# The value projections of mLSTM heads 0 and 1 joined into 512-column matmuls and moved behind the second FoX head pair's q and k

## The chip, the cores and the metric

The kernel runs on one core of one Trainium2 chip. The metric is the device time of the program in microseconds (us), the median of three runs. A profiled execution, taken separately, gives the trace that is read below. Engines are named as in the profile: PE is TensorE's matmul, PEld its weight load, DVE is VectorE, ACT is ScalarE, POOL is GpSimd, SP issues most DMAs.

## What is computed

One residual block on 512 tokens of width 1024. Cut to what matters here:

```python
proj = einsum('bsd,de->bse', h, w_in) + b_in        # h = LN(x) scaled and shifted
fq, fk, fv, ff, mu, mv, mi, mf, mo, ga, gb = split(proj)
att = forgetting_attention(fq, fk, fv, ff)          # FoX: 8 heads x 64, causal softmax
u  = silu(causal_conv(mu))
mq, mk = per head: u_head @ w_mq, u_head @ w_mk     # 4 heads, 256 -> 128
hm = mlstm_chunkwise(mq, mk, mv, mi, mf)            # 4 heads, v width 256
y  = (sigmoid(ga) * (att @ w_pa) + sigmoid(gb) * (head_norm(hm) * sigmoid(mo)) @ w_pb) @ w_out
```

followed by a layer norm and a SwiGLU of inner width 2816. `mv` is the value projection of the mLSTM branch: 512 x 1024 (tokens by d_model) times 1024 x 256 for each of four heads.

## The kernel before

Every float32 product is made of three matmuls on values split into a high and a low part: `mm3` issues hi x hi (L186), hi x lo (L189) and lo x hi (L190) into one PSUM bank. Weights come in chunks of 128 x 1024 (512 KB): `emit_chunk` issues the load on SP (L152, tile `raw`, three buffers), ACT casts the high part (L157, `whi`, four buffers), DVE subtracts it to make the low part (L161, `wlo`, four buffers). Chunks are taken in the order of the list `PLAN`, three ahead of their use, so a chunk's number (`whi17`, `raw17`) is its place in that list.

The stretch that the change touches is the FoX phase (about 77 to 222 us). For each FoX head `fox_scores` makes four score tiles `fs{h}_{qb}` of 128, 256, 384 and 512 keys (L641 to L643, computed at least 256 wide) in the two PSUM banks named `s`. DVE reads each into SBUF with the forget bias and the row minimum (L646, tile `L{h}_{qb}`), which frees the bank, ACT takes the exponential (L648), DVE the reciprocal of the sum (L649), ACT scales (L650). `fox_out` transposes the tiles on PE (L663), ACT copies them (L665, `pT`) and PE multiplies with `v` (L671, `fo`).

Projections fill PE between these steps. They are generators in the list `queue`: `prep_u(h)` (mu and the convolution), `prep(h)` (the values of an mLSTM head, then its `mqk`), `fm_unit` (a block of fq, fk, mo). `fill(n)` runs the next n pieces of the first ones. All projections, and `mqk`, write to the two PSUM banks named `acc`, so a unit waits until DVE or ACT has read the unit before the last out of its bank. For fq that is two ACT copies (L301) and two DVE subtractions (L302, tiles `ql`), one for each head of the pair; for fk the same (L310, L311). The tiles of q and k of a head have two buffers, so the pair 2 overwrites the pair 0.

`prep(0)` makes, for each of four token blocks, 8 x 3 matmuls with 256 moving columns (the head's value width), adds the bias on DVE (L614, `vt`) and splits the sum into `vxh` and `vx`. After the FoX phase `ml_scores` loads a row of `rowd` broadcast over partitions (tile `nb`, issued by ACT, L704) and the mLSTM phase follows.

The code's order is not the order on the engines: the framework's scheduler places every instruction, from the dependences and its own idea of time. The rows of both programs are therefore shown with the change.

Of the kernel before, what the change touches and what calls it, by code (L numbers as in the profile page):

```python
# [8 lines left out]
F32 = mybir.dt.float32  # L9
# [3 lines left out]
ALU = mybir.AluOpType  # L13
# [3 lines left out]
P = 128  # L17
D = 1024
S = 512
KT = 8  # L20
# [22 lines left out]
def plan():  # L43
    out = [("start", k) for k in range(KT)]
    out += [("gv", j) for j in range(4)]

    def mu(h):
        return [("mu", 2 * h), ("mu", 2 * h + 1)]

    def mvqk(h):  # L50
        return [("mv", 2 * h), ("mv", 2 * h + 1), ("mqk", h)]

    out += mvqk(0)
    out += [("fq", 2), ("fk", 2)]
    out += mu(1) + mvqk(1)
    out += [("fq", 3), ("fk", 3)]
    out += mu(2)
    out += [("mo", 0), ("mo", 1)]
    out += mu(3)
    out += [("mo", 2), ("mo", 3)]  # L60
    out += mvqk(2)
    out += [("mo", 4), ("mo", 5)]
    out += mvqk(3)
    out += [("mo", 6), ("mo", 7)]
    for f in range(8):
        out += [("ga", f), ("gb", f), ("pa", f)]
        if f > 0:
            out += [("pb", f - 1)]
    out += [("pb", 7)]
    out += [("wo", k) for k in range(KT)]  # L70
    for f in range(FT):
        out += [("fg", f), ("fu", f)]
    for q in range(4):
        out += [("dn", q * 6 + j) for j in range(6)]
    return out
# [25 lines left out]
def block_kernel(ctx, tc, x, c, wada, wpk, cols, gvb, mvb, lnp, out):  # L101
    nc = tc.nc
    V, A, G, T = nc.vector, nc.scalar, nc.gpsimd, nc.tensor
# [27 lines left out]
    offs = {}  # L131
# [4 lines left out]
    st = {"n": 0, "tiles": {}, "resident": {}}  # L136
    AHEAD = 3

    def w_off(key):

        if key[0] in ("gv", "mv") or key in (("fg", 0), ("fu", 0), ("fg", 1), ("fu", 1)):
            return 0
        return 16

    def emit_chunk(i):
        key = PLAN[i]
        w = chunk_width(key)
        if key in (("wo", 6), ("wo", 7), ("fu", 1), ("fg", 2)):
            raw = adap.tile([P, VW], F32, tag="adaw", name=f"raw{i}", bufs=2)
        else:  # L150
            raw = stp.tile([P, CW], F32, tag="raw", name=f"raw{i}", bufs=3)
        st["dma"] = nc.sync.dma_start(raw[:, :w], wpk[offs[key]:offs[key] + P * w].rearrange("(p w) -> p w", p=P))  # L152
        if key in st["resident"]:
            hi, lo = st["resident"][key]
        else:
            hi, lo = (stp.tile([P, CS], F32R, tag=t_, name=f"{t_}{i}")[:, w_off(key):w_off(key) + w] for t_ in ("whi", "wlo"))
        st["hi"] = A.copy(hi[:, :w], raw[:, :w])  # L157
        if key in LATE_LO:
            late.append((lo[:, :w], raw[:, :w], hi[:, :w]))
        else:  # L160
            (G if key in POOL_LO else V).tensor_tensor(lo[:, :w], raw[:, :w], hi[:, :w].bitcast(F32), ALU.subtract)  # L161
        st["tiles"][key] = (hi, lo)
# [16 lines left out]
    def get(key, ahead=AHEAD):  # L179
        prefetch(key, ahead)  # L180
        return st["tiles"].pop(key)

    def mm3(ps, lhs, rhs, first, last, pin=False):
        lh, ll = lhs
        rh, rl = rhs
        m = T.matmul(ps, lh, rh, start=first, stop=False)  # L186
        if pin:
            tc.keep_in_program_order(m)
        T.matmul(ps, lh, rl, start=False, stop=False)  # L189
        T.matmul(ps, ll, rh, start=False, stop=last)  # L190

    def split(hi, lo, src):
        A.copy(hi, src)  # L193
        V.tensor_tensor(lo, src, hi.bitcast(F32), ALU.subtract)
# [41 lines left out]
    def acc_tile(name):  # L236
        return ps.tile([P, S], F32, tag="acc", name=name)
# [119 lines left out]
    for hf in range(2):  # L357
        s_ = slice(hf * S, hf * S + S)
# [25 lines left out]
    for tb in range(TB):  # L384
        xt = xts[tb]
        mv = small.tile([P, 2], F32, tag="lnmv", name=f"xmv{tb}")
# [14 lines left out]
        for h in range(2 if tb == TB - 1 else 1):  # L401
            s_ = slice(h * S, h * S + S) if tb == TB - 1 else slice(0, D)
# [10 lines left out]
    for k in range(KT):  # L413
        pt = pts[k]
        sc, sh = mods[:, 2 * k:2 * k + 1], mods[:, 2 * k + 1:2 * k + 2]
        if k == 0:
            w = start_conv(0)
# [8 lines left out]
        hi, lo = w  # L426
        if k + 1 < KT:
            w = start_conv(k + 1)
# [11 lines left out]
    mla_s, mla = scope(name="mla", bufs=2)  # L440
# [12 lines left out]
    def hk(k, sl=slice(0, S)):  # L453
        return hhi[:, k, sl], hlo[:, k, sl]
# [15 lines left out]
    queue = []  # L470
# [16 lines left out]
    mvt = {0: fox.tile([P, S], F32, tag="mvt", name="mvt0", bufs=1)}  # L487
# [68 lines left out]
    mq, mk, vx = {}, {}, {}  # L556
# [31 lines left out]
    def fm_unit(name, b):  # L588
        yield from gemm_fm(name, b)
        r = evac_fm(name, b, gemm_done.pop((name, b)))  # L590
        if name == "mo":
            mot[b] = r

    def prep_u(h):
        for i in range(2):
            b = 2 * h + i
            if b not in mup:
                yield from fm_unit("mu", b)
            conv(b)

    def prep(h):
        vl = mla.tile([P, TB, 258], F32R, tag="vx", name=f"vx{h}")
        vh = adap.tile([P, TB, 258], F32R, tag="adaw", name=f"vxh{h}", bufs=2)
        G.tensor_copy(vh[:, :, 256:258], ones[:, 0:2 * TB].rearrange("p (t o) -> p t o", o=2))
        G.tensor_copy(vl[:, :, 256:258], lfc[:, 0, 0:2 * TB].rearrange("p (t o) -> p t o", o=2))
        w0, w1 = get(("mv", 2 * h)), get(("mv", 2 * h + 1))
        for tb in range(TB):
            ps = acc_tile(f"mv{h}_{tb}")
            for k in range(KT):
                hi, lo = (w0, w1)[k // 4]  # L610
                s_ = slice((k % 4) * 256, (k % 4) * 256 + 256)
                mm3(ps[:, :256], hk(k, slice(tb * P, (tb + 1) * P)), (hi[:, s_], lo[:, s_]), k == 0, k == KT - 1)
            vt = mla.tile([P, 256], F32, tag="th", name=f"vt{h}_{tb}", bufs=1)
            V.tensor_tensor(vt, ps[:, :256], mvt[h // 2][:, (h % 2) * 256:(h % 2) * 256 + 256], ALU.add)  # L614
            split(vh[:, tb, 0:256], vl[:, tb, 0:256], vt)
            yield
        vx[h] = (vh, vl)
        hi, lo = get(("mqk", h))
        for i, dst in ((0, mq), (1, mk)):
            ps = acc_tile(f"mqk{h}_{i}")  # L620
            for k in range(2):
                s_ = slice((i * 2 + k) * P, (i * 2 + k + 1) * P)
                uh, ul = us[2 * h + k]
                mm3(ps, (hi[:, s_], lo[:, s_]), (uh, ul), k == 0, k == 1)
            t = mla.tile([P, S], F32, tag=f"qk{i}", name=f"qk{i}_{h}")
            A.copy(t, ps)
            dst[h] = t
        yield
# [44 lines left out]
                    tc.keep_in_program_order(m)  # L673

    mot = {}
    queue += [prep_u(0), prep(0), fm_unit("fq", 2), fm_unit("fk", 2), prep_u(1), prep(1)]
    queue += [fm_unit("fq", 3), fm_unit("fk", 3), prep_u(2), fm_unit("mo", 0), fm_unit("mo", 1), fm_unit("mu", 6), fm_unit("mu", 7)]
    fill(2)
    for p in range(NH // 2):
# [105 lines left out]
    for f in range(KT):  # L785
# [4 lines left out]
        hi, lo = get(("pa", f))  # L790
        for k in range(4):
            s_ = slice(k * P, (k + 1) * P)
# [302 lines left out]
    for f in range(NF0, FT):  # L1095
        b1, b26, b57, b34 = s_tile(f"p1_{f}"), acc_tile(f"p26_{f}"), o_tile(f"p57_{f}"), tr_tile(f"p34_{f}")
        h1, h2 = slice(0, HB), slice(HB, S)
        r = ftp.tile([P, 7, HB], F32, tag="r", name=f"r{f}", bufs=1)
# [171 lines left out]
```

## Time and profile before

| what | value |
|---|---|
| runs, us | 851.03, 851.63 (median), 855.49 |
| profiled execution, us | 852.84 |
| its span, us | 851.1 |
| mean granted clock of TensorE | 0.996 |
| PE busy | 828.2 us (97%) |
| PEld busy | 742.1 us (87%) |
| DVE busy | 597.9 us (70%) |
| ACT busy | 381.7 us (45%) |

Busy time is the time with an instruction in the engine. Matmuls are pipelined, so neighbouring ones overlap: a single matmul's busy time is longer than the distance between two starts. PE idles 22.9 us of the span.

### The profile page before, as it was taken

Reading aid. Unit: us, or ns where it says so; the run is one execution under the profiler, and the core shown is the slowest. Engines: PE = TensorE matmul, PEld = TensorE weight load, DVE = VectorE, ACT = ScalarE, POOL = GpSimd, SP = SyncE. Lnnn points to the kernel's source line nnn. Section 1 sums busy time; section 2 is a strip of 40 time slices with the busy share of each in tenths; the row PEclk is TensorE's granted clock in tenths of the full one; section 3 lists DMA queues with packets and bytes.
Section 4 is the critical chain, followed back from the end, with each engine's and each line's share of the span. In section 5 each row is a group of like instructions: output and inputs, shape, how many; then the busy total and the mean of one; then the engine's idle time right before and its main releaser. Section 6 shows DMA issues by size and latency. Waiting matters only on the chain.

```text
span 851.1 us, 14125 instructions
## 1 busy us (share of the span) xinstructions
PE 828.2 (97%) x5518; PEld 742.1 (87%) x5518; DVE 597.9 (70%) x1113; ACT 381.7 (45%) x606; POOL 80.6 (9%) x140
## 2 busy tenths in 40 slices
PE   6999999999889999999999999999999999999996
PEld 4889878777778888888888889999999999999996
DVE  7977546464387667776765898888888888744247
ACT  6555867674454333322243265644444444611110
POOL 2030000000021110000000221021111110000001
PEclk9999999999999999999999999999999999999999
DMA  9953331522212224876667216577877774522202
GB/s 351 371 163 99 125 100 66 145 75 62 94 57 75 75 75 155 282 258 239 242 234 256 114 50 174 141 193 189 196 176 174 195 191 131 179 88 99 95 30 100
DMA packets 46477, 130.08 MB, mean 153 GB/s; under 512 B 5293, under 2 KB 5693, under 8 KB 46410
## 3 DMA queue, kind: packets, MB, share of 16 engines
q1 hardware_dynamic: 37930, 113.97, 39.6%
q0 software_dynamic: 6752, 12.06, 8.4%
q10 hardware_dynamic: 1728, 3.15, 1.2%
q8 instruction: 43, 0.70, 0.3%
q14 instruction: 24, 0.20, 0.1%
HBM read 124.93 MB, written 2.13 MB: 149 GB/s over the span
## 4 chain that ended last, share of the span: by engine, by line
PE 91%; DVE 3%; DMA 1%; ACT 1%; issue 1%; POOL 0%; SPq 0%; DVEq 0%; ACTq 0%; POOLq 0%
PE p L189 7%; PE p L186 7%; PE p L190 7%; PE dn L186 5%; PE dn L189 5%; PE dn L190 5%; PE mo L186 2%; PE mo L189 2%; PE ga L190 2%; PE gb L186 2%; PE gb L190 2%; PE pb L190 2%; PE ga L186 2%; PE pb L186 2%; PE ga L189 2%; PE gb L189 2%
## 5 line engine op out<-in xcount | busy, mean ns | idle before, releaser
L161 DVE TENSOR_TENSOR wlo<-raw,whi 128x1024 fp32r<-128x1024 f32 (+2 forms) x94 | 106.3, 1136 | 109.0 <-ACT whi L157 101.8
L157 ACT CAST whi<-raw 128x1024 fp32r<-128x1024 f32 (+2 forms) x98 | 95.4, 980 | 179.7 <-PE dn L190 70.8
L189 PE MATMUL dn<-wlo,ah 128*128 128x256 f32 x352 | 97.3, 278 | 0.0
L186 PE MATMUL dn<-whi,ah 128*128 128x256 f32 x352 | 97.2, 278 | 0.1
L190 PE MATMUL dn<-whi,al 128*128 128x256 f32 x352 | 96.0, 278 | 0.0
L189 PE MATMUL p<-tlo,whiu 128*128 128x256 f32 x304 | 84.2, 277 | 0.0
L190 PE MATMUL p<-thi,wlou 128*128 128x256 f32 x304 | 84.2, 277 | 0.0
L186 PE MATMUL p<-thi,whiu 128*128 128x256 f32 x304 | 84.2, 277 | 0.0
L186 PEld LDWEIGHTS dn<-whi,ah 128*128 128x128 f32 x352 | 66.2, 188 | 0.3 <-ACT ah L193 0.3
L189 PEld LDWEIGHTS dn<-wlo,ah 128*128 128x128 f32 x352 | 66.2, 188 | 0.0
L190 PEld LDWEIGHTS dn<-whi,al 128*128 128x128 f32 x352 | 65.5, 188 | 0.0
L190 PE MATMUL p<-hhi,wlou 128*128 128x256 f32 x228 | 62.9, 276 | 0.0
L186 PE MATMUL p<-hhi,whiu 128*128 128x256 f32 x228 | 62.9, 276 | 0.0
L189 PE MATMUL p<-hlo,whiu 128*128 128x256 f32 x228 | 62.9, 276 | 0.0
L271 DVE CUSTOM_DVE_ANT_0 adaw<-adaw,cb 128x1024 f32<-128x1024 f32 x32 | 39.1, 1223 | 26.8 <-DMA adaw<-in_wada_dram 26.8
L190 PEld LDWEIGHTS p<-thi,wlou 128*128 128x128 f32 x304 | 57.2, 188 | 0.0
L189 PEld LDWEIGHTS p<-tlo,whiu 128*128 128x128 f32 x304 | 57.2, 188 | 0.0
L186 PEld LDWEIGHTS p<-thi,whiu 128*128 128x128 f32 x304 | 57.2, 188 | 0.0
L210 POOL TENSOR_TENSOR lnrs<-lnrs,mhalf 128x1 f32<-128x1 f32 x12 | 13.1, 1094 | 322.3 <-DVE lnrs L209 322.3
L193 ACT CAST whiu<-raws 128x1024 fp32r<-128x1024 f32 (+1 forms) x38 | 30.8, 832 | 28.6 <-DMA raws<-in_wpk_dram 14.9
L186 PEld LDWEIGHTS p<-hhi,whiu 128*128 128x128 f32 x228 | 42.8, 188 | 0.0
L190 PEld LDWEIGHTS p<-hhi,wlou 128*128 128x128 f32 x228 | 42.8, 188 | 0.0
(370 smaller groups left out, 2342.8 us busy)
## 6 DMA issues: line engine op xcount, KB each, us to landing
raw<-in_wpk_dram SPq DMA_DIRECT2D x84, 512.0 KB, 3.6
adaw<-in_wada_dram SPq DMA_DIRECT2D x48, 512.0 KB, 5.1
raws<-in_wpk_dram SPq DMA_DIRECT2D x57, 256.0 KB, 3.8
rawg<-in_wpk_dram SPq DMA_DIRECT2D x19, 512.0 KB, 3.9
raws<-in_wpk_dram POOLq DMA_DIRECT2D x38, 256.0 KB, 6.1
raw<-in_wpk_dram SPq DMA_DIRECT2D x16, 256.0 KB, 2.7
raw<-in_wpk_dram SPq DMA_DIRECT2D x8, 384.0 KB, 9.3
raw<-in_wpk_dram SPq DMA_DIRECT2D x4, 528.0 KB, 8.1
```

The costliest lines, as they stand in the source:

```text
L157: st["hi"] = A.copy(hi[:, :w], raw[:, :w])
L161: (G if key in POOL_LO else V).tensor_tensor(lo[:, :w], raw[:, :w], hi[:, :w].bitcast(F32), ALU.subtract)
L186: m = T.matmul(ps, lh, rh, start=first, stop=False)
L189: T.matmul(ps, lh, rl, start=False, stop=False)
L190: T.matmul(ps, ll, rh, start=False, stop=last)
L193: A.copy(hi, src)
L210: G.tensor_tensor(rs, rs, mhalf, ALU.pow)
L271: V.tensor_tensor_reduce(wt, wt, cb, 1.0, 0.0, ALU.mult, ALU.add, t)
```

## The change

The values of heads 0 and 1 are made together: `prep_v01` loads four weight chunks, each holding two of the eight k tiles for both heads side by side (two half-chunk DMAs of 256 KB each, 512 columns per k tile), and makes 8 x 3 matmuls with 512 moving columns for each token block, two token blocks at a time in both `acc` banks. That is 96 matmuls of 512 columns in place of 192 of 256. The bias add covers both heads at once (4 of 512 columns in place of 8 of 256); the splits stay 8 on ACT and 8 on DVE of 256 columns. `prep(0)` and `prep(1)` lose their value part and keep `mqk` as `prep_qk`. The queue and `PLAN` are put in another order: fq and fk of pair 2 come first, then `mqk` of head 0, mu of head 1, the joined values and `mqk` of head 1. Heads 2 and 3 keep their code.

```diff
--- before.py
+++ after.py
@@ -50,9 +50,8 @@
     def mvqk(h):
         return [("mv", 2 * h), ("mv", 2 * h + 1), ("mqk", h)]
 
-    out += mvqk(0)
-    out += [("fq", 2), ("fk", 2)]
-    out += mu(1) + mvqk(1)
+    out += [("fq", 2), ("fk", 2), ("mqk", 0)]
+    out += mu(1) + [("mv", j) for j in range(4)] + [("mqk", 1)]
     out += [("fq", 3), ("fk", 3)]
     out += mu(2)
     out += [("mo", 0), ("mo", 1)]
@@ -138,7 +137,7 @@
 
     def w_off(key):
 
-        if key[0] in ("gv", "mv") or key in (("fg", 0), ("fu", 0), ("fg", 1), ("fu", 1)):
+        if key[0] == "gv" or key[0] == "mv" and key[1] > 3 or key in (("fg", 0), ("fu", 0), ("fg", 1), ("fu", 1)):
             return 0
         return 16
 
@@ -149,7 +148,16 @@
             raw = adap.tile([P, VW], F32, tag="adaw", name=f"raw{i}", bufs=2)
         else:
             raw = stp.tile([P, CW], F32, tag="raw", name=f"raw{i}", bufs=3)
-        st["dma"] = nc.sync.dma_start(raw[:, :w], wpk[offs[key]:offs[key] + P * w].rearrange("(p w) -> p w", p=P))
+        if key[0] == "mv" and key[1] < 4:
+
+            j, c0 = divmod(key[1], 2)
+            r = raw[:, :w].rearrange("p (k h d) -> p k h d", k=2, h=2)
+            for h in range(2):
+                o_ = offs[("mv", 2 * h + j)]
+                src = wpk[o_:o_ + P * w].rearrange("(p k d) -> p k d", p=P, k=4)
+                st["dma"] = nc.sync.dma_start(r[:, :, h, :], src[:, 2 * c0:2 * c0 + 2, :])
+        else:
+            st["dma"] = nc.sync.dma_start(raw[:, :w], wpk[offs[key]:offs[key] + P * w].rearrange("(p w) -> p w", p=P))
         if key in st["resident"]:
             hi, lo = st["resident"][key]
         else:
@@ -598,11 +606,38 @@
                 yield from fm_unit("mu", b)
             conv(b)
 
-    def prep(h):
+    def v_tiles(h):
         vl = mla.tile([P, TB, 258], F32R, tag="vx", name=f"vx{h}")
         vh = adap.tile([P, TB, 258], F32R, tag="adaw", name=f"vxh{h}", bufs=2)
         G.tensor_copy(vh[:, :, 256:258], ones[:, 0:2 * TB].rearrange("p (t o) -> p t o", o=2))
         G.tensor_copy(vl[:, :, 256:258], lfc[:, 0, 0:2 * TB].rearrange("p (t o) -> p t o", o=2))
+        vx[h] = (vh, vl)
+        return vh, vl
+
+    def prep_v01():
+
+        ts = [v_tiles(h) for h in range(2)]
+        w = [get(("mv", j)) for j in range(4)]
+        for t2 in range(2):
+            pss = [acc_tile(f"mv01_{t2 * 2 + i}") for i in range(2)]
+            for j in range(4):
+                hi, lo = w[j]
+                for i in range(2):
+                    tb = 2 * t2 + i
+                    for k in (2 * j, 2 * j + 1):
+                        s_ = slice((k % 2) * S, (k % 2) * S + S)
+                        mm3(pss[i], hk(k, slice(tb * P, (tb + 1) * P)), (hi[:, s_], lo[:, s_]), k == 0, k == KT - 1)
+                if j % 2:
+                    yield
+            for i in range(2):
+                tb = 2 * t2 + i
+                vt = mla.tile([P, S], F32, tag="th", name=f"vt01_{tb}", bufs=1)
+                V.tensor_tensor(vt, pss[i], mvt[0], ALU.add)
+                for h in range(2):
+                    split(ts[h][0][:, tb, 0:256], ts[h][1][:, tb, 0:256], vt[:, h * 256:h * 256 + 256])
+
+    def prep(h):
+        vh, vl = v_tiles(h)
         w0, w1 = get(("mv", 2 * h)), get(("mv", 2 * h + 1))
         for tb in range(TB):
             ps = acc_tile(f"mv{h}_{tb}")
@@ -614,7 +649,9 @@
             V.tensor_tensor(vt, ps[:, :256], mvt[h // 2][:, (h % 2) * 256:(h % 2) * 256 + 256], ALU.add)
             split(vh[:, tb, 0:256], vl[:, tb, 0:256], vt)
             yield
-        vx[h] = (vh, vl)
+        yield from prep_qk(h)
+
+    def prep_qk(h):
         hi, lo = get(("mqk", h))
         for i, dst in ((0, mq), (1, mk)):
             ps = acc_tile(f"mqk{h}_{i}")
@@ -673,7 +710,7 @@
                     tc.keep_in_program_order(m)
 
     mot = {}
-    queue += [prep_u(0), prep(0), fm_unit("fq", 2), fm_unit("fk", 2), prep_u(1), prep(1)]
+    queue += [prep_u(0), fm_unit("fq", 2), fm_unit("fk", 2), prep_qk(0), prep_u(1), prep_v01(), prep_qk(1)]
     queue += [fm_unit("fq", 3), fm_unit("fk", 3), prep_u(2), fm_unit("mo", 0), fm_unit("mo", 1), fm_unit("mu", 6), fm_unit("mu", 7)]
     fill(2)
     for p in range(NH // 2):
```

In the rows below a name's last number is the scheduler's tile number; `fs1_2` is the score tile of head 1, query block 2; lines after L158 stand 8 to 37 lines further on in the changed file (L641 there is L678).

On PE, where the second FoX head's score tiles stand: before, they lie between matmuls of `mv0_3` and `mqk0_0`.

```order
L186 MATMUL mv0_3_1090<-whi13_889,hhi_84 128x256
L189 MATMUL mv0_3_1090<-wlo13_890,hhi_84 128x256
L190 MATMUL mv0_3_1090<-whi13_889,hlo_85 128x256
L641 MATMUL fs1_1_1057<-k1_0_565,qh1_0_556 128x256
L642 MATMUL fs1_1_1057<-k1_0_565,ql1_0_557 128x256
L643 LDWEIGHTS identb_537
L643 MATMUL fs1_1_1057<-maskb_539,identb_537 128x128
L186 MATMUL mv0_3_1090<-whi13_889,hhi_84 128x256
L189 MATMUL mv0_3_1090<-wlo13_890,hhi_84 128x256
L190 MATMUL mv0_3_1090<-whi13_889,hlo_85 128x256
L186 MATMUL mqk0_0_1125<-uhi0_861,whi14_895 128x512
L189 MATMUL mqk0_0_1125<-ulo0_862,whi14_895 128x512
```

In the changed program the 24 matmuls of fq2 stand where mv0_0 began, then fk2; behind fk2's last matmul eight score tiles follow each other, four rows each, from fs0_2 to fs2_1, and then `mqk0_0`. The last of the eight rows by row:

```order
L679 MATMUL fs1_3_1038<-k1_0_565,ql1_0_557 128x512
L680 LDWEIGHTS identb_537
L680 MATMUL fs1_3_1038<-maskb_539,identb_537 128x128
L678 MATMUL fs2_0_1181<-k0_1_580,qh0_1_568 128x256
L679 MATMUL fs2_0_1181<-k0_1_580,ql0_1_569 128x256
L680 LDWEIGHTS identb_537
L680 MATMUL fs2_0_1181<-maskb_539,identb_537 128x128
L678 MATMUL fs2_1_1192<-k0_1_580,qh0_1_568 128x256
L679 MATMUL fs2_1_1192<-k0_1_580,ql0_1_569 128x256
L680 LDWEIGHTS identb_537
L680 MATMUL fs2_1_1192<-maskb_539,identb_537 128x128
L194 MATMUL mqk0_0_1074<-uhi0_861,whi14_891 128x512
```

The matmuls that stood between score tiles have moved ahead of them or behind them.

On DVE, for the same stretch of the changed program, from the reading of fs0_2 to the subtraction `ql1_2` that reads fq2's bank for the last time (row-minimum reads and reciprocals stand between, four reciprocals in all, and aren't shown; chunk 17 is the first of the four joined value chunks):

```order
L683 ISA L0_2_954,mx0_2_955<-fs0_2_950,fb0_926 128x384
...
L683 ISA L0_3_965,mx0_3_966<-fs0_3_961,fb0_926 128x512
...
L169 TENSOR_TENSOR wlo17_1071<-raw17_1067,whi17_1070 128x1024
L683 ISA L1_0_1009,mx1_0_1010<-fs1_0_1005,fb1_1003 128x128
...
L310 SCALAR_TENSOR_TENSOR ql0_2_973<-fq2_901,colt_69,qh0_2_972 64x512
L683 ISA L1_1_1020,mx1_1_1021<-fs1_1_1016,fb1_1003 128x256
...
L319 SCALAR_TENSOR_TENSOR k0_2_1061<-fk2_990,colt_69,k0_2_1061 64x512
...
L683 ISA L1_2_1031,mx1_2_1032<-fs1_2_1027,fb1_1003 128x384
...
L683 ISA L1_3_1042,mx1_3_1043<-fs1_3_1038,fb1_1003 128x512
...
L310 SCALAR_TENSOR_TENSOR ql1_2_979<-fq2_901,colt_69,qh1_2_978 64x512
```

Before, fq2's subtractions stood behind all score tiles of heads 0 and 1; now one stands between those of head 1 and one behind them, and the bank that `mqk0_0` writes is fq2's.

On PE, at the end of the FoX phase, before, from the last matmuls of mo3 to the mLSTM values of head 2:

```order
L186 MATMUL mo3_2387<-hhi_84,whi31_2209 128x512
L189 MATMUL mo3_2387<-hlo_85,whi31_2209 128x512
L663 MATMUL ft7_3_2158<-ident_60,L7_3_2016 128x128
L671 MATMUL fo3_2069<-pT6_2_2142,v_593 64x256
L671 MATMUL fo3_2069<-pT7_2_2137,v_593 64x256
L663 MATMUL ft6_3_2162<-ident_60,L6_3_1958 128x128
L190 MATMUL mo3_2387<-hhi_84,wlo31_2210 128x512
L671 MATMUL fo3_2069<-pT6_3_2164,v_593 64x128
L671 MATMUL fo3_2069<-pT7_3_2160,v_593 64x128
L186 MATMUL mv2_0_2480<-whi32_2243,hhi_84 128x256
```

And in the changed program:

```order
L198 MATMUL mo3_2283<-hhi_84,wlo31_2106 128x512
L700 MATMUL ft7_2_2030<-ident_60,L7_2_1901 128x128
L700 MATMUL ft7_2_2030<-ident_60,L7_3_1912 128x128
L708 MATMUL fo3_1965<-pT6_1_2026,v_593 64x384
L708 MATMUL fo3_1965<-pT7_1_2020,v_593 64x384
L700 MATMUL ft6_2_2035<-ident_60,L6_2_1843 128x128
L700 MATMUL ft6_2_2035<-ident_60,L6_3_1854 128x128
L700 MATMUL ft7_3_2054<-ident_60,L7_3_1912 128x128
L708 MATMUL fo3_1965<-pT6_2_2038,v_593 64x256
L708 MATMUL fo3_1965<-pT7_2_2033,v_593 64x256
L700 MATMUL ft6_3_2058<-ident_60,L6_3_1854 128x128
L708 MATMUL fo3_1965<-pT6_3_2060,v_593 64x128
```

One matmul of mo3 stood between the transpose ft6_3 and the `fo` that uses it; now mo3 is finished ahead of the whole group, and no projection stands between a transpose and its `fo`.

## Rows read from the trace of the kernel before

**Rows 1.** Windows: us, then PE, PEld, DVE, ACT, POOL busy; PEclk, DMA share, GB/s.

```profile
77.00:95.00 18.00, 18.00 (x139) 16.46 (x138) 14.35 (x39) 11.53 (x29) 0.00 (x0) 1.00 0.54 172
...
230.00:250.00 20.00, 17.18 (x113) 15.46 (x113) 16.59 (x62) 10.62 (x21) 4.96 (x14) 0.91 0.08 29
```

**Rows 2.** Waits of PE, 60 to 310 us: total us, times, longest.

```profile
PE mv L186 <- DVE vt L614: 2.4, 1, 2.4
PE mv L186 <- ACT mo L323: 1.8, 1, 1.8
...
PE ft L663 <- ACT L L650: 0.4, 1, 0.4
```

**Rows 3.** Groups of instructions by shape on PE: busy us, mean ns, idle before.

```profile
L189 PE MATMUL mv<-wlo,hhi 128*128 128x256 f32 x128 | 37.0, 289 | 0.0
...
L186 PE MATMUL wo<-woh,yhi 128*128 128x512 f32 x32 | 12.4, 389 | 0.0
```

**Rows 4.** Timeline of PE, matmuls of 256 and of 512 columns: start, busy us.

```profile
84.56 0.28 PE L189 MATMUL mv<-wlo,hhi 128*128 128x256 f32 x1
...
86.92 0.28 PE L186 MATMUL mv<-whi,hhi 128*128 128x256 f32 x1
...
105.18 0.40 PE L190 MATMUL fk<-hhi,wlo 128*128 128x512 f32 x1
...
108.59 0.39 PE L190 MATMUL fk<-hhi,wlo 128*128 128x512 f32 x1
```

**Rows 5.** Timeline of PE, score tiles and what follows them.

```profile
84.00 0.36 PE L641 MATMUL fs<-k,qh 128*128 128x256 f32 x1
...
84.36 0.36 PE L186 MATMUL mv<-whi,hhi 128*128 128x256 f32 x1
...
87.03 0.34 PE L641 MATMUL fs<-k,qh 128*128 128x384 f32 x1
...
87.43 0.48 PE L641 MATMUL fs<-k,qh 128*128 128x512 f32 x1
...
88.02 0.36 PE L189 MATMUL mv<-wlo,hhi 128*128 128x256 f32 x1
```

**Rows 6.** Timeline of DVE, 77 to 113 us, one instruction of each kind.

```profile
84.66 0.28 DVE L646 CUSTOM_DVE_ANT_0 L<-fs,fb 128x128 f32<-128x128 f32 x1
...
84.86 0.42 DVE L646 CUSTOM_DVE_ANT_0 L<-fs,fb 128x256 f32<-128x256 f32 x1
...
87.66 0.56 DVE L646 CUSTOM_DVE_ANT_0 L<-fs,fb 128x384 f32<-128x384 f32 x1 [0.93 <-PE fs L643]
...
88.25 0.69 DVE L646 CUSTOM_DVE_ANT_0 L<-fs,fb 128x512 f32<-128x512 f32 x1
...
94.39 1.22 DVE L161 TENSOR_TENSOR wlo<-raw,whi 128x1024 fp32r<-128x1024 f32 x1
95.53 0.16 DVE L649 RECIPROCAL sm<-sm 128x1 f32<-128x1 f32 x1
...
104.47 0.74 DVE L302 SCALAR_TENSOR_TENSOR ql<-fq,colt,qh 64x512 fp32r<-64x512 f32 x1
```

**Rows 7.** Timeline of PE, end of the FoX phase.

```profile
221.85 0.44 PE L671 MATMUL fo<-pT,v 128*64 128x128 f32 x4 [0.28 <-ACT pT L665]
```

**Rows 8.** Chain of waits, the piece behind the FoX phase: start, us.

```profile
223.00 5.22 DMA nb<-rowd
```

**Rows 9.** Landing times of the DMAs that read rowd (fb, nb), whole program.

```profile
DMA to landing us min/median/max: 3.0/3.8/5.4
```

**Rows 10.** Timeline of PE at the lower clock, behind the idle time of 2.4 us.

```profile
243.85 0.41 PE L189 MATMUL mv<-wlo,hhi 128*128 128x256 f32 x1
...
246.41 0.41 PE L189 MATMUL mv<-wlo,hhi 128*128 128x256 f32 x1
```

**Rows 11.** SP's weight loads ahead of the FoX phase, and landings of raw, 76 to 100 us.

```profile
78.98 2.05 SPq L152 DMA_DIRECT2D raw<-in_wpk_dram  x2
...
DMA to landing us min/median/max: 2.7/3.2/5.5
```

## The prediction

> **What bounds the kernel now.** I read the windows first. Between 77 and 95 us, where the first score tiles and the values of head 0 stand, PE is busy for 18.00 of 18.00 us at a granted clock of 1.00; DVE is busy for 14.35 and ACT for 11.53 [rows 1]. So PE sets the time there, but DVE has less than 4 us in 18 to spare: the reader should keep that number, since the change moves work of DVE too. The list of waits then says that PE waits hardly anywhere: from 60 to 310 us its longest waits are 2.4 and 1.8 us for the value tiles of later heads and 0.4 us for a scaled score tile [rows 2]. A change in the FoX phase can therefore win in two ways only, by fewer PE microseconds or by one of these waits, and it can lose by any new wait of PE.
>
> **What the wide matmuls save.** The groups by shape seem to promise a lot: a 256-column value matmul is busy for 289 ns, a 512-column one for 389 ns [rows 3], so 192 x 0.289 - 96 x 0.389 = 55.5 - 37.3 = 18.1 us. That reading is wrong as long as matmuls follow each other, for they overlap. Distances between starts count. From 84.56 to 86.92 there are 20 steps of 256 columns: 2.36 / 20 = 0.118 us. From 105.18 to 108.59 there are 15 steps of 512 columns: 3.41 / 15 = 0.2273 us [rows 4]. So 192 x 0.118 = 22.66 becomes 96 x 0.2273 = 21.82: **-0.84 us**. The Trainium skill, "TensorE: Matmul & The Clock Gate", section "Back-to-back issue gap", gives a sustained spacing of about 81 ns at 128 columns and 131 ns at 512; between them an estimate for 256 is 98 ns, and the merge would then save 192 x 0.098 - 96 x 0.131 = 6.2 us. The trace does not agree: its 512-column spacing is 227 ns, not 131.
>
> **What the new order costs: a stall on DVE.** In the changed program fq2 takes the place of mv0_0, at the start of the first window, and behind fk2 eight score tiles stand in a row on PE, with no projection between them, and then mqk0_0. Its bank is fq2's, and that is free only when DVE has done ql1_2. On DVE the readings of fs0_2 to fs1_3, the subtraction of chunk 17 and three halves of the q and k of pair 2 stand ahead. The chain from the end of fs0_2 on PE is therefore:
>
> First the hand-over to DVE: before, fs0_2 ends where fs0_3 starts, 87.43 [rows 5], and DVE starts at 87.66 [rows 6]: 0.23 us. Then 14 instructions by their busy times [rows 6]: readings of 384 and 512 (0.56, 0.69), the 128x1024 subtraction (1.22), a reading of 128 (0.28), ql0_2 (0.74), a reading of 256 (0.42), k0_2 (0.74: no row of its own is shown, it has ql's shape), reading of 384 (0.56), reading of 512 (0.69), four reciprocals (0.15 each, its row 0.16), and ql1_2 (0.74): 7.24 us. Starts lie closer than that: 94.39 to 95.53 is 1.14 for a subtraction that is busy 1.22, 84.66 to 84.86 is 0.20 for a reading that is busy 0.28 [rows 6], 0.08 less each. With 13 such overlaps, 7.24 - 1.04 = 6.20 us.
>
> PE has from the same moment only the score tiles fs0_3, fs1_0, fs1_1, fs1_2, fs1_3, fs2_0 and fs2_1. By starts a 256-wide tile takes 84.36 - 84.00 = 0.36, the 384-wide 87.43 - 87.03 = 0.40, the 512-wide 88.02 - 87.43 = 0.59 [rows 5]: 4 x 0.36 + 0.40 + 2 x 0.59 = 3.02 us. PE thus stands for 0.23 + 6.20 - 3.02 = 3.41 us, and the way back from DVE to PE adds some 0.1: **+3.5 us**. Bounds: 3.2 if PE's hand-over were free, 4.45 if the busy times don't overlap. ACT has the cast of chunk 17, three copies of fq2 and fk2 and four exponentials in the same stretch; I take them as hidden behind DVE, and if they are not, the upper end covers it. What DVE did there before, the additions and splits of head 0's values, moves behind, where PE has 512-column work to cover it. PE cannot win the stall back, since before it was busy all through [rows 1] and the work is the same.
>
> **Smaller terms.** The wait of 0.4 us for a scaled tile [rows 2] falls where other units now stand between: **-0.4**, at worst 0. At the end of the FoX phase the last `fo` waits 0.28 us for `pT` [rows 7] although one mo3 matmul of 0.23 stands between its transpose and it; the full round trip is 0.51. In the changed program two such round trips stand uncovered, but for the transpose ft7_3 (some 0.07): 2 x 0.51 - 0.07 - 0.28 = **+0.7**, at best 0. Then the nb transfer takes 5.22 us on the chain [rows 8], while transfers from rowd land in 3.8 us at the median and 3.0 at best [rows 9]. The scheduler's order on SP now puts a weight load ahead of mvt instead of behind it, so nb meets less of it: between 0 and 5.22 - 3.8 = 1.4 us less; I take not quite half, **-0.6**. The bias adds (4 of 512 columns for 8 of 256) on DVE and the doubled DMA issues on SP lie on engines that nobody waits for there: nothing, as long as the loads land in time (below). The filler of the mLSTM phase keeps its units.
>
> **The sum.** -0.84 + 3.5 - 0.4 + 0.7 - 0.6 = +2.4 us, so the profiled 852.84 would become 855.2, and the median 851.63, 1.21 below that execution, **854.0 us**. With all bounds it is 851.63 + (-0.84 + 3.2 - 0.4 + 0 - 1.4) = 852.2 to 851.63 + (-0.84 + 4.45 + 0.7) = 855.9.
>
> **Rivals.**
>
> *The stall also costs the clock (slower yet).* After the wait of 2.4 us before mv [rows 2] matmuls of 256 columns start 2.56 / 12 = 0.213 us apart, from 243.85 to 246.41 [rows 10], which is half of 2.4 GHz; the window's granted clock is 0.91 [rows 1]. Some 15 matmuls at 0.095 us more is 1.4 us. The stall here is longer, but broken up by score tiles, so I hold it less likely than not: 854.0 + 1.4 = 855.4 us.
>
> *The loads of chunk 17 come late (slower).* It comes in two half DMAs, and its cast stands on ACT ahead of the copies of fq2 and fk2, its subtraction on DVE in the chain above. With fq2 at the start of the first window and two score tiles ahead of fs0_2, PE reaches the end of fk2 not before 77 + 48 x 0.2273 + 2 x 0.36 = 88.6; the cast cannot start earlier, since it takes fk2's buffer. A landing later than about 89 costs one for one, and from 91 on the result is over 0.5% slower, 856 to 858 us. For it: two DMAs in place of one, in pieces of a quarter of the length. Against it: SP issues loads at this place by 81.03, and they land within 2.7 to 5.5 us [rows 11], so by 86.5.
>
> *The stall does not come (no change or a little faster).* If the hand-overs on DVE are shorter or mqk0_0 finds its bank free: 851.63 - 0.84 - 0.4 + 0.7 - 0.6 = 850.5 us. It needs ql1_2 done 3.4 us earlier than the order on DVE allows.
>
> *The wide matmuls run nearer to their busy times (faster).* If 512 columns stepped at less than two 256-column steps by more than the fk rows show, the gain lies between 0.84 and 18.1 us; with a saving half way, 9.5, the result is 854.0 - 8.6 = 845.4 us. Every row of 512 columns in a stream speaks against it [rows 4]. This is also the side on which the page's spacing lies.
>
> **How the numbers follow.** Chances: the stall as summed 0.60; with the fall of the clock 0.18; late loads 0.08; no stall 0.10; cheaper wide matmuls 0.04. The likeliest is 854.0 us. The range 850.3 to 856.7 holds the first, the second and the fourth, 0.88, less their own spread. A measurement of this kernel tells some 0.5% from no change, 4.3 us: faster means below 847.4, slower above 855.9. Faster: the last rival, 0.04, and what I may have overlooked, 0.02. Slower: late loads 0.08, a third of the second, 0.06, and the upper tail of the first, 0.06. That leaves 0.74 for the same.
>
> **What would show it.** In the profile after: 512-column mv matmuls 0.227 us apart; about 3.4 us of PE waits between 88 and 97, for DVE's L and ql (one group of them before mqk0); PE's busy time in a window of 77 to 95 well below its length; the wait of 2.4 us before a later mv still there, and nb landing in 4 to 5 us. I am wrong if PE's busy time there stays whole, if mv steps fall below 0.2 us, or if a later stretch, which the order leaves as it was, changes by more than 1 us.

## The result, and the profile after

The changed kernel takes 858.2 us in the median of 9 runs (855.75 to 860.96), against 851.72 us for the kernel before: the ratio on record is 1.0061, with a 95% interval of 1.0042 to 1.0079, so it is slower by 3.6 to 6.7 us (the two medians alone would give 1.0076). The forecast was 854.0 us with a range up to 856.7; the time lies outside it. The profiled execution takes 857.58 us with a span of 855.9, 4.8 us more than before.

The windows of the changed kernel show where to look (columns as in [rows 1]):

```profile
85.00:95.00 10.00, 8.17 (x40) 5.78 (x38) 6.19 (x23) 6.98 (x19) 1.02 (x2) 0.95 0.63 192
95.00:110.00 15.00, 15.00 (x61) 12.04 (x62) 4.76 (x12) 10.44 (x22) 1.02 (x2) 0.80 0.34 79
...
230.00:250.00 20.00, 16.56 (x124) 14.96 (x123) 14.79 (x57) 9.69 (x21) 5.56 (x16) 1.00 0.14 45
```

Before, PE was busy without a break from 77 to 95 us at full clock [rows 1]. Now it is idle for 1.83 us between 85 and 95, and in the next 15 us it is busy all the time, but at a granted clock of 0.80. A busy share of 100% hides that loss; the clock column shows it. In the window from 230 to 250 it is the other way round: the 0.91 of before has become 1.00.

PE's waits in the changed kernel, 60 to 330 us (total us, times, longest), beside [rows 2]:

```profile
PE mv L194 <- DVE vt L649: 1.9, 1, 1.9
PE fs L678 <- DVE mx L683: 1.6, 3, 0.8
PE ms L749 <- DVE E L750: 1.5, 1, 1.5
PE mv L194 <- ACT mo L331: 1.5, 1, 1.5
PE fo L708 <- ACT pT L702: 0.4, 1, 0.4
```

The second line is new: score tiles wait for DVE's readings. PE's timeline from the end of fs0_2 to mqk of head 0:

```profile
89.57 0.47 PE L678 MATMUL fs<-k,qh 128*128 128x512 f32 x1
...
92.47 0.44 PE L678 MATMUL fs<-k,qh 128*128 128x384 f32 x1 [0.77 <-DVE mx L683]
...
93.47 0.50 PE L678 MATMUL fs<-k,qh 128*128 128x512 f32 x1 [0.32 <-DVE mx L683]
...
94.91 0.58 PE L678 MATMUL fs<-k,qh 128*128 128x256 f32 x1 [0.53 <-DVE mx L683]
...
95.64 0.58 PE L678 MATMUL fs<-k,qh 128*128 128x256 f32 x1
...
96.50 0.79 PE L194 MATMUL mqk<-uhi,whi 128*128 128x512 f32 x1
97.09 0.63 PE L197 MATMUL mqk<-ulo,whi 128*128 128x512 f32 x1
...
100.50 0.56 PE L194 MATMUL mqk<-uhi,whi 128*128 128x512 f32 x1
```

and DVE's, the first reading of the stretch, the subtraction of chunk 17, the readings of fs1_0 and fs1_3, and the instruction that frees fq2's bank:

```profile
89.80 0.56 DVE L683 CUSTOM_DVE_ANT_0 L<-fs,fb 128x384 f32<-128x384 f32 x1
...
90.99 1.22 DVE L169 TENSOR_TENSOR wlo<-raw,whi 128x1024 fp32r<-128x1024 f32 x1
92.13 0.28 DVE L683 CUSTOM_DVE_ANT_0 L<-fs,fb 128x128 f32<-128x128 f32 x1
...
94.90 0.67 DVE L683 CUSTOM_DVE_ANT_0 L<-fs,fb 128x512 f32<-128x512 f32 x1
...
95.69 0.76 DVE L310 SCALAR_TENSOR_TENSOR ql<-fq,colt,qh 64x512 fp32r<-64x512 f32 x1
```

DVE starts 0.23 us after fs0_2 and ends ql1_2 at 96.45; mqk0 starts at 96.50, 6.93 us behind fs0_2's end at 89.57. The score tiles need 3.02 of them, so PE lost 3.9 us. (The windows count only 1.83 us as idle, since the busy time of a matmul reaches past the moment at which the next one could start.)

Where in the row the 3.9 us lie is seen by laying the starts of the score tiles beside the ends of DVE's readings. The tiles share the two banks `s`, so each can start only when DVE has read the tile two before it. fs1_2 starts at 92.47, DVE ends the 128-wide reading of fs1_0 at 92.13 + 0.28 = 92.41; fs2_1 starts at 95.64, DVE ends the 512-wide reading of fs1_3 at 94.90 + 0.67 = 95.57. All tiles from fs1_0 on start 0.06 or 0.07 us behind such an end. Only the last step, from fs2_1 to mqk0, can belong to fq2's bank: 0.86 us in place of 0.36, so 0.50 of the 3.9 at most. The waits say the same: 1.6 us for readings of score tiles (`mx`), none for `ql`. PE thus goes at DVE's pace through the whole row.

Then come the steps of mqk0: from 97.09 to 100.50 eight steps of 512 columns take 3.41 us, 0.426 each, where full clock gives 0.227 [rows 4]. The clock is at half until about 100.9, so that the 12 matmuls of mqk0 take 4.9 us in place of 2.7.

The joined values do step as summed. Eleven steps in 2.50 us:

```profile
121.69 0.39 PE L198 MATMUL mv<-whi,hlo 128*128 128x512 f32 x1
...
124.19 0.40 PE L198 MATMUL mv<-whi,hlo 128*128 128x512 f32 x1
```

At the end of the FoX phase no filler stands between the transposes and their `fo`:

```profile
222.96 0.39 PE L198 MATMUL mo<-hhi,wlo 128*128 128x512 f32 x1
...
226.47 0.44 PE L708 MATMUL fo<-pT,v 128*64 128x128 f32 x4 [0.35 <-ACT pT L702]
228.43 0.39 PE L194 MATMUL mv<-whi,hhi 128*128 128x256 f32 x1 [1.53 <-ACT mo L331]
```

### The profile page after: what moved, and what is told of

Its sections match the earlier page's. It is cut to its first block, busy times and chain, and to the rows that moved or that the text cites. A ratio compares the mean times of both kernels' runs of the same rounds, so it can differ in the third digit from the quotient of the medians.

```text
span 855.9 us, 13936 instructions
## 1 busy us (share of the span) xinstructions
PE 829.6 (97%) x5422; PEld 737.4 (86%) x5422; DVE 597.9 (70%) x1109; ACT 380.2 (44%) x606; POOL 80.5 (9%) x140
## 4 chain that ended last, share of the span: by engine, by line
PE 93%; DVE 2%; ACT 1%; DMA 1%; issue 1%; DVEq 0%; POOL 0%; ACTq 0%
PE p L194 7%; PE p L198 7%; PE p L197 7%; PE dn L197 5%; PE dn L194 5%; PE dn L198 5%; PE mo L194 2%; PE mo L198 2%; PE mo L197 2%; PE ga L198 2%; PE ga L197 2%; PE gb L198 2%; PE pb L198 2%; PE gb L197 2%; PE pb L197 2%; PE ga L194 2%
## 5 line engine op out<-in xcount | busy, mean ns | idle before, releaser
L197 PEld LDWEIGHTS p<-hlo,whiu 128*128 128x128 f32 x228 | 42.8, 188 | 0.0
```

## The experiments

To compare kernels I divide PE's timeline of each profile into three parts: **A**, from the last gv matmul to the last fo (before: 77.41 to 221.85); **B**, from there to the mv that waits for DVE's vt in the mLSTM phase (243.47, [rows 2]); **C**, from there to the first ga matmul (299.15). Behind it the kernels have the same order, and yet it took 551.8 us in one kernel's profile and 558.8 in another's, a difference larger than the effects here. The verdict therefore rests on the ratios to the kernel before, and the parts, which come from one profile of each kernel, say where the time lies. Kernels that the table leaves out have their ratios in the text.

| kernel | A | B | C | sum | ratio (95% interval) |
|---|---|---|---|---|---|
| before | 144.44 | 21.62 | 55.68 | 221.74 | 1 |
| changed | 149.65 | 21.47 | 54.34 | 225.46 | 1.0061 (1.0042 to 1.0079) |
| order_only | 148.69 | 19.61 | 54.17 | 222.47 | 1.0016 (1.0000 to 1.0031) |
| v_first | 150.78 | 21.50 | 54.26 | 226.54 | 1.0062 (1.0040 to 1.0084) |
| warm | 147.65 | 20.95 | 54.34 | 222.94 | 1.0027 (1.0010 to 1.0043) |
| order_warm | 146.49 | 19.60 | 54.18 | 220.27 | 0.9988 (0.9972 to 1.0004) |
| after_tail | 149.37 | 20.13 | 54.24 | 223.74 | 1.0030 (1.0009 to 1.0051) |
| tail_warm | 147.30 | 20.43 | 55.80 | 223.53 | 1.0026 (1.0012 to 1.0039) |
| after_t | 147.82 | 19.83 | 55.82 | 223.47 | 1.0043 (1.0028 to 1.0058) |
| before_t | 143.43 | 19.74 | 54.24 | 217.41 | 0.9971 (0.9952 to 0.9989) |

**The order or the join?** First each half of the change alone. `order_only` takes the kernel before and changes `PLAN` and the queue; `prep` keeps its 256 columns. Of the edit only the queue's line is shown, as in all diffs below where the order changes:

```diff
-    queue += [prep_u(0), prep(0), fm_unit("fq", 2), fm_unit("fk", 2), prep_u(1), prep(1)]
+    queue += [prep_u(0), fm_unit("fq", 2), fm_unit("fk", 2), prep_qk(0), prep_u(1), prep(0), prep(1), prep_qk(1)]
```

> The new order alone: fq2, fk2 and mqk of head 0 come first, but the values of heads 0 and 1 stay separate, with 192 matmuls of 256 columns and whole-chunk loads. Theory A (the order makes the loss): the same eight score tiles stand in a row, mqk0 starts about 19.5 us after fq2, matmuls behind it run at half clock until about 101 us; the time is that of the changed kernel plus 0.84, a ratio of 1.005 to 1.009 to before (856 to 859.5 us). Theory B (the joined loads and wide tiles make the loss): no such stall, ratio 0.998 to 1.002.

Its ratio is 1.0016. The stall is there to the hundredth: mqk0 starts 19.56 us behind fq2, as in the changed kernel, and runs at half clock:

```profile
95.58 0.79 PE L185 MATMUL mqk<-uhi,whi 128*128 128x512 f32 x1
96.17 0.63 PE L188 MATMUL mqk<-ulo,whi 128*128 128x512 f32 x1
...
100.44 0.44 PE L189 MATMUL mqk<-uhi,wlo 128*128 128x512 f32 x1
```

So theory A was right on the place and wrong on the total, which is where theory B had it: part A is 4.3 us longer than before, but B and C together are 3.5 us shorter (1.5 of them in C, where the clock falls in the profile of the kernel before and not in this one; see below). `v_first` is the other half, the joined values in the old place of head 0's (head 1's come earlier than before):

```diff
-    queue += [prep_u(0), fm_unit("fq", 2), fm_unit("fk", 2), prep_qk(0), prep_u(1), prep_v01(), prep_qk(1)]
+    queue += [prep_u(0), prep_v01(), prep_qk(0), fm_unit("fq", 2), fm_unit("fk", 2), prep_u(1), prep_qk(1)]
```

> The joined 512-column values alone, in the old place, ahead of mqk0, fq2 and fk2. Theory A: no row of score tiles without filler, no half clock near 95 us, ratio 0.997 to 1.001 (849 to 852.5 us), unless the four chunks that are now needed at once at 77 us come late. Theory B: ratio 1.004 or more.

1.0062, against my expectation. There is no stall near 95 us, but one at 138, where with head 1's values already done nothing is left to stand between the score tiles of heads 3 and 4:

```profile
138.20 0.39 PE L678 MATMUL fs<-k,qh 128*128 128x256 f32 x1 [0.61 <-DVE mx L683]
...
140.31 0.72 PE L194 MATMUL mqk<-uhi,whi 128*128 128x512 f32 x2 [0.60 <-ACT uhi L201]
...
142.37 0.63 PE L198 MATMUL mqk<-uhi,wlo 128*128 128x512 f32 x1
142.80 0.63 PE L197 MATMUL mqk<-ulo,whi 128*128 128x512 f32 x1
```

again with half clock behind it (0.43 us a step). That nothing is left there is read from its order, not tried. The joined values thus lose without the new order, and the order alone loses 0.0016, at the edge of the noise (1.0000 to 1.0031). The join costs 0.0045 beside the new order.

**The clock as a price of its own.** `warm` is the changed kernel with matmuls whose results are not used, in the gaps ahead of fs1_2 and fs1_3:

```diff
+    WARM = {(1, 1): 6, (1, 2): 3}
...
+            if (h, qb) in WARM:
+                wt = tr_tile(f"warm{h}_{qb}")
+                for _ in range(WARM[(h, qb)]):
+                    last = after(T.matmul(wt[:, 0:256], qh[:, 0:P], kt[:, 0:256], start=True, stop=True), last)
```

> The changed kernel with nine extra matmuls of 256 columns into an unused bank, six between fs1_1 and fs1_2 and three between fs1_2 and fs1_3, where PE idles for 0.8 and 0.3 us; their results are not used. Theory A with the clock as a separate price: mqk0 starts no earlier than in the changed kernel (19 to 20 us after fq2), but its matmuls step by 0.23 us instead of 0.43, and the time is 2 to 2.7 us less than that of the changed kernel (about 855.5 us). Rival: the clock falls anyway or costs nothing, the time is that of the changed kernel (858 us) or more.

```profile
85.00:95.00 10.00, 8.99 (x49) 6.58 (x47) 6.57 (x23) 7.19 (x18) 1.53 (x3) 1.00 0.59 140
```

```profile
90.64 0.96 PE L688 MATMUL warm<-k,qh 128*128 128x256 f32 x6
...
95.63 0.50 PE L194 MATMUL mqk<-uhi,whi 128*128 128x512 f32 x1 [0.29 <-DVE ql L310]
95.97 0.40 PE L197 MATMUL mqk<-ulo,whi 128*128 128x512 f32 x1
...
98.31 0.39 PE L198 MATMUL mqk<-uhi,wlo 128*128 128x512 f32 x1
```

mqk0 starts no earlier (19.54 us behind fq2) and steps by 0.23. The ratio falls by 0.0034, 2.9 us; part A by 2.0. The same matmuls in the kernel with the order alone:

> The new order with separate values, and the nine extra matmuls between the score tiles of head 1 that keep PE busy. If the half clock is a price of its own, it comes on top: 2.0 to 2.7 us below the kernel with the order alone, 850.5 to 851.5 us, ratio 0.998 to 1.000 to before. Rival: no gain, 853.

0.9988: 0.0028 less than `order_only`. Shown twice: the half clock behind the stall costs 2.0 to 2.9 us, and extra work without use is faster here than idling. The granted clock of whole executions, on record for every run, agrees: its mean is 0.992 over the nine runs of the changed kernel and 0.996 over the twelve of `warm`, 0.994 for `order_only` and 0.997 for `order_warm`, and 0.995 over 126 runs of the kernel before.

**Taking the stall away.** `o_banks` accumulates fq2 and fk2 in other PSUM banks:

```diff
-        ps = acc_tile(f"{name}{b}")
+        ps = (o_tile if (name, b) in (("fq", 2), ("fk", 2)) else acc_tile)(f"{name}{b}")
```

> The changed kernel, but fq2 and fk2 are accumulated in the two PSUM banks of the fox output, so that mqk0 does not wait for the reading of fq2. Theory A: projections stand between the score tiles again, the stall and the half clock go, 5 to 6 us less than the changed kernel: 851 to 853 us. Rival (DVE's amount of work in that stretch is the limit, not the bank): PE still waits 3 us or more between 88 and 100 us, time 856 or more.

1.0051 (1.0034 to 1.0069). The scheduler answered with another order: mqk0 went ahead of fq2, and projections stand between the score tiles again. The stall is gone, against the rival:

```profile
90.00:100.00 10.00, 10.00 (x47) 8.08 (x46) 5.81 (x16) 7.62 (x17) 1.02 (x2) 1.00 0.42 121
```

But the time did not fall, against theory A: PE waited 1.4 us for the scan of DVE at 78, the clock fell at 80 us and again at 226, and transposes waited 1.7 us for ACT. `order_tr` moves mqk of head 0 to the transposes' banks in the kernel with the order alone, and `tail_tr` in the changed kernel (with the filler of `after_tail`, below). First `order_tr`, then `tail_tr`:

```diff
-            ps = acc_tile(f"mqk{h}_{i}")
+            ps = (tr_tile if h == 0 else acc_tile)(f"mqk{h}_{i}")
```

> The new order with separate values, and mqk of head 0 accumulated in the two banks of the transposes, which are free until ft1_0. It then stands ahead of fs0_3 and does 2.7 us of real work while DVE reads the score tiles. Theory A (stall of 3.9 us on fq2's bank plus half clock of 2.2): the stall falls to about 1.2, no half clock near 95 us: 4 to 5 us below the kernel with the order alone, ratio 0.996 to 0.998. Rival (the next unit, mu2, waits for the same bank as long): at most the 2 us of the clock, ratio 0.999 or more.

> The changed kernel (joined values) with mqk of head 0 in the banks of the transposes and the held-back mo3 matmuls: both losses repaired. Ratio 0.996 to 0.999 if they add up as summed; if the joined values cost something of their own beside the end of the FoX phase, 0.999 to 1.001 and slower than the separate ones by 0.0015 or more.

1.0037 (1.0016 to 1.0058), so no gain, and 1.0030 (1.0015 to 1.0045), slower than either of its two expectations. mqk0 went ahead of fs0_3, and the other score tiles, now behind it, still follow each other in a row. Waits of `order_tr`:

```profile
PE fs L644 <- DVE mx L649: 2.4, 4, 1.0
...
PE mu L185 <- DVE ql L301: 0.3, 1, 0.3
```

The rival for `order_tr` was right on the time and not on the reason: the next unit, mu2, waits only 0.3 us for fq2's bank, and 2.4 us go to readings of score tiles. In `tail_tr` these are again 2.4 us, and mu2 shows no wait. Another bank for mqk0 does not help, because the row waits for its own banks; `o_banks` lost the stall when projections stood between the tiles.

The last way is an order in which fq2 and fk2 come behind mqk0 and mu2, mu3, first with separate values (`mu_first_sep`), then with joined ones (`mu_first`):

```diff
+    queue += [prep_u(0), prep_qk(0), prep_u(1), fm_unit("fq", 2), fm_unit("fk", 2), prep(0), prep(1), prep_qk(1)]
```

> Separate values in 256 columns; mqk of head 0 and mu of head 1 come ahead of fq2 and fk2, so that the reading of fq2 falls where other banks serve, and projections stand between the score tiles of heads 0 and 1; the values come behind. Theory A: no stall near 90 us, the gain of the new order in the mLSTM stretch (about 3.5 us) is kept: 847 to 850 us, ratio 0.995 to 0.998. Rival (that gain belongs to the late start, not to the order): 851 to 852.

> The same order with the joined 512-column values. By starts the join saves 0.8 us; by theory C it loses 3 to 4 at the end of the FoX phase, where no filler is left: 850 to 853 us, slower than with separate values by 2 to 4 us. Rival (the joined values cost nothing but for the stall): as fast as the separate ones or 0.8 us faster.

1.0002 (0.9983 to 1.0021) with separate and 1.0029 (1.0014 to 1.0044) with joined values. The stall is gone (part A is 144.90 with separate values, near that of before); PE waits 1.2 us at 78 to 81 instead, for DVE's Mr and em (0.3 and 0.9). The join costs 0.0027 in this order too, about as much as the intervals allow for noise. By parts that loss lies ahead of the last fo: A is 148.05 with joined values, with mo3 used up at 213.9 and PE waiting 1.7 us for ACT between 216 and 219; B and C hardly differ.

**The end of the FoX phase.** In the orders of all joined kernels mo3 is used up before the last transposes; in the separate ones it stands between them. `after_tail` holds mo3 back in the changed kernel, its k tiles (eight, of three matmuls each) from 1 on behind the transposes ft6_2, from 5 on behind ft6_3; `mu_first_tail` does the same in `mu_first`, and `tail_warm` adds the extra matmuls of `warm`. The expectations follow in this order; the diff is cut to the lines that matter:

```diff
+    TAIL = {1: (6, 2), 5: (6, 3)}
...
+            if (name, b) == ("mo", 3) and k in TAIL:
+                after(m, st[("ft", *TAIL[k])])
```

> The changed kernel, with nothing moved but the filler at the end of the FoX phase: 12 matmuls of mo3 are held back until behind the transposes ft6_2 and 9 until behind ft6_3, so that they stand between a transpose and its fo as they do in the kernel with the order alone. Theory C (what the joined values cost beside the order comes from the end of the FoX phase, where the scheduler has used up mo2 and mo3 too early): the 5.2 us from the last mo3 matmul to the first mv of head 2 lose 1.5 to 2 us, the mLSTM stretch up to ga another 1 to 2, the time is 2 to 4 us below the changed kernel (854 to 856). Rival (the joined values cost in their own stretch): within 1 us of the changed kernel.

> The joined values in the order with mqk of head 0 and mu of head 1 ahead of fq2 and fk2, and the mo3 matmuls held back to the end of the FoX phase. Theory C: the join's loss in this order (ratio 1.0029 against 1.0002) goes, ratio 0.999 to 1.001. Rival: it stays at 1.0025 or more.

> The changed kernel with both repairs that leave its order alone: nine extra matmuls between the score tiles of head 1 (clock) and the held-back mo3 matmuls at the end of the FoX phase (filler). If the two prices are separate they add: 1.0061 - 0.0034 - 0.0031, a ratio of 0.9996 (0.998 to 1.001). Rival (one cause seen twice): 1.0025 to 1.003, as with either alone.

`after_tail` is 0.0031 below the changed kernel; 1.3 of the 1.7 us by parts lie in B. `mu_first_tail` reaches 1.0024 (1.0008 to 1.0041) and `tail_warm` 1.0026: no gain that can be told apart from the kernels without it. In `mu_first_tail` the waits only moved, to 0.18, 0.28 and 0.68 us between 214 and 217, ahead of the matmuls held back. In `tail_warm` the table shows where the expected sum fails: A and B are shorter than in the changed kernel by 2.4 and 1.0, but C is 55.80 like before, 1.5 more. Behind the mv that waits for vt the clock fell again (granted 0.70 at 244 to 246, 0.50 in the next 2 us). In the table C is 55.7 to 55.8 where it falls there and 54.2 to 54.3 where it doesn't. The length of the wait doesn't settle it: 2.4 us ahead of a fall in `before`, `tail_warm`, `order_tr` and `mu_first_tail`, 2.0 in `after_t` and `mfs_t`, but 2.4 and 2.5 without one in `after_tail` and `order_t2`.

**Work behind the last fo.** `order_only` has three mo3 matmuls behind it. `before_t` and `after_t` bring this to the kernels before and after: nine matmuls of mo3 are held back behind ft6_2, nine behind ft6_3 and the last three behind the last fo. `order_t2` does it in `order_only` with six, six and nine, `mfs_t` in `mu_first_sep` with nine, nine and three. The line for all but `order_t2`, then the expectations in this order:

```diff
+    TAIL = {1: ("ft", 6, 2), 4: ("ft", 6, 3), 7: ("fo", 3, 3)}
```

> The kernel before with nothing changed but the place of mo3's last 21 matmuls: 9 behind ft6_2, 9 behind ft6_3, 3 behind the last fo. If work behind the last fo counts: the stretch from the last fo to the mv that waits for vt shrinks from 21.6 to 20 us or less, ratio 0.996 to 0.999. Rival: unchanged, 0.999 to 1.001.

> The changed kernel with mo3's last matmuls in the same places. If work behind the last fo counts: that stretch falls from 21.5 to about 19.6 us, as in the kernel with the order alone, and the ratio from 1.0061 to 1.0015 to 1.003. Rival: as with the filler ahead of the last fo only, 1.003 or more.

> The new order with separate values, and nine mo3 matmuls behind the last fo instead of three. If work there is free because a chain of DMA, ACT and DVE sets that stretch: 1 to 1.4 us less than the kernel with the order alone, ratio 1.000 (0.9985 to 1.0015). Rival: the last fo then waits for its transposes longer, nothing gained.

> The order without the stall (mqk of head 0 and mu of head 1 ahead of fq2 and fk2, values separate, ratio 1.0002) with mo3's last matmuls held back, 3 of them behind the last fo. If both reasons hold: no fall of the clock behind the last fo, that stretch under 20 us: ratio 0.995 to 0.998, faster than both kernels. Rival: 0.999 to 1.001.

`before_t`, which is the kernel before with only these 21 matmuls moved, is the fastest of all: 849.16 us, 0.9971, and its interval lies below 1:

```profile
220.41 0.44 PE L676 MATMUL fo<-pT,v 128*64 128x128 f32 x4
...
221.35 0.40 PE L190 MATMUL mo<-hhi,wlo 128*128 128x512 f32 x1
222.66 0.38 PE L186 MATMUL mv<-whi,hhi 128*128 128x256 f32 x1 [0.91 <-ACT mo L324]
240.15 0.39 PE L186 MATMUL mv<-whi,hhi 128*128 128x256 f32 x1 [1.99 <-DVE vt L619]
```

No wait for pT stands ahead of the last fo, the wait of 1.8 us [rows 2] is 0.91, B is 1.9 us shorter and the clock doesn't fall behind the mv. By parts 1.9 us of its gain lie in B, 1.0 in A and 1.4 in C. `after_t` has B at 19.83 but had the fall; its 1.0043 is the rival's, no clear gain over the changed kernel or `after_tail`. `order_t2` with nine gained nothing (1.0036, 1.0020 to 1.0051), the rival again. `mfs_t` is 0.9993 (0.9977 to 1.0009), the rival's too and no better than `mu_first_sep` by more than the intervals; its profile has B at 19.80 and the fall (C 55.99). So the edit clearly helps in one kernel of three with three matmuls behind the last fo. How much of that gain belongs to these three and how much to the 18 ahead of them was not separated, and why it fails elsewhere is open.

## Why the prediction was wrong

- **The merge, -0.84.** Right as a sum of starts: 0.227 us a step. The 18 us of the busy times are refuted by the same rows, and no run bears out the spacing at 512 columns that the Trainium skill gives in "TensorE: Matmul & The Clock Gate", section "Back-to-back issue gap": 131 ns there, 227 here. But the join was not free beside it: against the order alone it costs 0.0045, against the same order without a stall 0.0027. By parts (1.0 us in A, 1.9 in B) two thirds of it lie behind the last fo in the new order, and holding back mo3 gives 0.0031 back there; in the order of `mu_first` the loss lies in A and holding back gives nothing clear. That the scheduler uses mo3 up earlier when the values are joined is read from its rows; why it does so was not tried, so the join's price is measured but its cause is only in part shown.
- **The stall, +3.5.** Right in place and size, 3.9 us, and in the DVE chain that sets it (0.23 to hand over, ql1_2 ending 6.65 us after DVE's start; I had 6.20; the way back, for which I had no row and put 0.1, took 0.05). The bank was wrong: I let PE run through the score tiles and stand at mqk0 for fq2's bank, but at least 3.4 of the 3.9 us lie at the score tiles, which wait for DVE to empty the two `s` banks. The size comes out alike, since in both pictures mqk0 stands behind ql1_2. The difference shows in what helps: another bank for mqk0 does not (`order_tr`, `tail_tr`).
- **"The stall also costs the clock", chance 0.18, +1.4.** This step failed. I held it less likely than not because score tiles break the stall up, and priced it at 15 matmuls of 256 columns, at the steps of [rows 10]. The clock did fall, in spite of the score tiles, and stayed at half for some 6 us over longer matmuls; `warm` and `order_warm` put its price at 2.0 to 2.9 us. Put into the likeliest case, the forecast would have been about 856.5, within the measured interval of 855.3 to 858.4 (851.72 times the ratio's bounds). That agreement is in part luck, since the join's price was not in the sum and the gain in C was not either.
- **The wait of 0.44 at 135.** Gone, as said.
- **The junction, +0.7, and nb, -0.6.** Part A is longer by 5.21; without 3.9 of stall, 2.15 of clock, -0.84 and -0.44 there is 0.4 left for the junction. nb took 4.79 us instead of 5.22, -0.4, and B is shorter by 0.15. Both small terms had the right sign. One wait of before I passed over in [rows 2]:

```profile
PE ms L712 <- DVE E L713: 0.7, 1, 0.7
```

It is 1.5 us in the changed kernel, 0.9 longer, which takes back what the waits for mo and vt lost (0.3 and 0.5).
- **What was not in the sum.** Behind the mv that waits for vt the clock no longer falls in the changed kernel, -1.3 us in part C: by more than the 1 us that I had named for a later stretch as a sign of being wrong. Up to the first ga the profile's loss is 225.46 - 221.74 = 3.7 us. The span's 4.8 are these 3.7, less 0.6 because the last gv matmul came earlier, and 1.7 behind ga, where nothing was changed: 1.4 of them in one idle time at 728 us that some profiles show and others don't. I don't count them as the change's.

## What to carry to other kernels

Taking the projections out from between units that share two PSUM banks puts the engine that must empty these banks onto the path: before doing so, add up what stands on that engine up to the last instruction that PE needs, and what other work PE has meanwhile. Lay the starts on PE beside the ends on the other engine for every bank, to see which one holds PE up. Price a new wait with the clock that follows it, and read the granted clock beside the busy share. Ask where the filler ends: spreading one projection's last 21 matmuls over the end of the FoX phase gained 0.3% in the kernel before, though nothing clear in two other orders.

## What the runs showed of the hardware

The granted clock fell to half, 1.2 GHz, although PE was never idle for longer than 0.8 us at a stretch: in the changed kernel PE was busy for 8.17 of 10.00 us between 85 and 95, and about 6 us at half clock followed, most of them through matmuls without a gap. With nine matmuls in the gaps (8.99 of 10.00 us busy) it stayed at 1.00. After the wait for vt it fell in six kernels' profiles and not in the others, with waits of 2.0 to 2.4 us ahead of a fall and 1.9 to 2.5 without one. The scatter of a few us between executions of one kernel is for the most part something else: over 126 runs of the kernel before, time and mean granted clock (0.992 to 0.998) go together only weakly (the correlation of the time with the time lost to the clock is 0.28).
